# A hybrid decoder layer: gate one-hots on VectorE turned by ScalarE, gate products laid out key by token, and a gather rate of 0.8 in the second mixer half

## The chip, the cores and the metric

The kernel runs on one core of one Trainium2 chip. The metric is the device time of one execution in microseconds (us); the kernel before takes 3289.25 us (median of 3 runs, 3288.27 to 9417.04).

## The reference, cut to what matters

One decoder layer on 1024 tokens of width 1024, in float32:

```
z   = x @ W_in                                  # LRU input and gate, GLA q k v and gate, merge gates
m   = sigmoid(gA) * (RG-LRU(z) * gelu(z_y)) + sigmoid(gB) * (RMSNorm(GLA(z)) * silu(z_r))
x   = LN1(alpha * x + m @ W_out)
ple = sigmoid(x @ W_pg) * (p @ W_pp)
x   = LN2(alpha * x + PEER(x) + ple)
```

PEER has 8 heads. Each token's query picks, in each head, the top 16 of 128 keys in two halves, then the top 16 of the 256 pairs; a pair (i, j) names one of 16384 experts. Expert e adds g_e * v_e * gelu(u_e . x), where g is a softmax over the 16 picked. So every token has 128 experts, each with a row of 1024 numbers in the tables u and v.

## The kernel before, in words

The 1024 tokens are 8 tiles of 128, in two halves of 4 tiles. For each half `mixer` runs the projections, the LRU and the GLA, and `post` runs the output projection, LN1, the queries, the scores of the keys and the ple gates. PEER is computed in two ways. For four tiles (0, 1, 6, 7, `GT`) the picked rows are gathered from HBM: `gather_u` fetches one row per token (128 rows for one of the 128 picks) and one VectorE operation multiplies it with x and sums (line 849); `gather_v` fetches for one token its 128 value rows, and TensorE multiplies four tokens' rows with block-diagonal weights `w32`, in 8 phases of 16 gathers a tile. For the other four tiles (4, 5, 2, 3, `DT`) all 16384 experts are computed: `dense` runs u, gelu, a gate for every expert and v, as three products each (`mm3`) of numbers split into a high and a low part (`split`: ScalarE writes the high part, VectorE subtracts).

The gates of the dense tiles come from `dense_gates`. A token's 128 picks lie on the partitions. For each token `one` marks the picked i-key, `oi` is `one` times the gate, `oj` marks the picked j-key, and the product of `oj` and `oi` over the picks is the token's table of gates, j by i. 16 tokens are collected in `gst` and stored. Before the change VectorE makes `one` and `oj` for 8 tokens at a time, ScalarE makes `oi` token by token, and ScalarE evicts four tokens' products from PSUM with a turn from token-key to key-token order.

The order of work. Gathers, routes and value products are a stream (`gathers`) that weaves u, routes and v one after the other. The code of the main work calls `pump(t)`, which adds t times a rate to a credit and issues steps of the stream while the credit is positive (a gather costs 1.46, a route's selection 1.0 a key list). `RATE` has the rate for the first post, the second mixer half, the second post and the dense stage. Routes join the weave once 100 u gathers are issued (`ROUTE`), and v of a tile once its u are done. A planner then orders each engine's instructions at compile time from modelled times and priorities; in the second mixer half the stream is held behind the last VectorE instruction issued (`PIN`) and has a lower priority, in the dense stage a much higher one (`LATER`). Row buffers are a ring of 7, in the dense stage 11, for u and v together. All gathers are issued on GpSimd's (POOL's) queue, all other loads and stores on SP's. `GATES` says how many blocks of 16 tokens of dense gates are issued in each step of the second post: two after each of four column blocks of the output projection, one after each of the eight heads, four before each of four column blocks of the ple gate.

Weights are used by both halves. `weights` splits them in the first half and stores the low part in HBM for the first 60 keys (`LOW`); in the second half those low parts are loaded, and the others split again. By the order of the calls the 60 keys are all of the mixer's 56 and the first 4 of the output projection's 8; those of the queries (8), the ple gate (8) and the ple projection (4) are not stored.

Of the kernel before, what the change touches and what calls it, by code (L numbers as in the profile page):

```python
# [8 lines left out]
F32 = mybir.dt.float32  # L9
F32R = mybir.dt.float32r  # L10
BF16 = mybir.dt.bfloat16
I32 = mybir.dt.int32
U32 = mybir.dt.uint32
AF = mybir.ActivationFunctionType
# [4 lines left out]
P = 128  # L19
# [22 lines left out]


ROUTE = 100
RATE = (0.8, 0.6, 1.0, 1.2)

V = mybir.EngineType.DVE
PIN = ((), (V,), (), (None,))
# [5 lines left out]
KG = 4  # L54
RING = 6

LOW = 60

TG = 8

# [7 lines left out]
def kernel(ctx: ExitStack, tc: tile.TileContext, a: dict, out: bass.AP, tap=None):  # L68
# [198 lines left out]
    def weights(src, name, shape):  # L267
# [8 lines left out]
        if low.get(key) is not None:  # L276
            nc.sync.dma_start(l.bitcast(F32), low[key])
            nc.scalar.activation(h, raw, AF.Copy)
        else:
            split(h, l, raw)  # L280
            if key not in low:
                n = len(low)
                low[key] = None
                if n < LOW:
                    low[key] = dram.tile(shape, F32, name=f"low{n}")
                    nc.sync.dma_start(low[key], l.bitcast(F32))
        return h, l

    low = {}
# [567 lines left out]
    def gather_v(ti, idx, idxT, gate, H):  # L857
# [5 lines left out]
        for ph in range(32 // N):  # L863

            w32 = peer.tile([P, 4, N, 32], F32, name="w32", bufs=2)
            nc.vector.memset(w32, 0.0)
            for c in range(4):
                dst = w32[:, c].rearrange("p r e -> p (r e)")[:, ph * N:ph * N + (N - 1) * 33 + 1:33]
                nc.vector.tensor_copy(dst, pw[:, 32 * c + ph * N:32 * c + ph * N + N])
            for r in range(N):  # L870

                rows_v = []
# [89 lines left out]
    def dense_gates(n, g_b, gps, iota):  # L962
# [2 lines left out]
        o = gps.tile([P, 4, KEYS], F32, name="pk3", tag="g")  # L965
        for j in range(3):
            nc.tensor.transpose(o[:, j], K3[:, j], ident)
        T3 = g_b.tile([P, 3, P], F32, name="T3", bufs=2)
        nc.scalar.activation(T3, o[:, :3], AF.Copy)
        Tb = g_b.tile([P, 2, P], BF16, name="Tb", bufs=2)  # L970
        nc.scalar.activation(Tb, o[:, :2], AF.Copy)
        for tb in range(P // 16):
            gs = g_b.tile([P, KEYS, 16], F32, name="gst", tag="g")
            for q in range(16 // TG):
                t0 = tb * 16 + q * TG
                tt = slice(t0, t0 + TG)
                B3 = [P, TG, KEYS]
                one = g_b.tile(B3, BF16, name="one", bufs=2)
                nc.vector.tensor_tensor(one, iota, Tb[:, 0, tt, None].to_broadcast(B3), op=ALU.is_equal)  # L979
                oj = g_b.tile(B3, F32, name="oj", bufs=2)  # L980
                nc.vector.tensor_tensor(oj, iota, Tb[:, 1, tt, None].to_broadcast(B3), op=ALU.is_equal)  # L981
                for r4 in range(TG // 4):
                    o = gps.tile([P, 4, KEYS], F32, name="pg", tag="g")
                    for r in range(4):
                        t = 4 * r4 + r
                        oi = g_b.tile([P, KEYS], F32, name="oi", bufs=6)
                        nc.scalar.activation(oi, one[:, t], AF.Copy, scale=T3[:, 2, t0 + t:t0 + t + 1])  # L987
                        nc.tensor.matmul(o[:, r], oj[:, t], oi, start=True, stop=True)  # L988
                    q4 = q * TG + 4 * r4
                    nc.scalar.activation(gs[:, :, q4:q4 + 4].rearrange("p i t -> p t i"), o, AF.Copy)  # L990
                    pump(0.9)
            nc.sync.dma_start(g_d[:, :, n * P // 16 + tb].rearrange("g j i t -> j g (i t)"),
                              gs.rearrange("p (g i) t -> p g (i t)", i=8))
            yield
# [109 lines left out]
    with ExitStack() as gctx:  # L1104
        g_b = gctx.enter_context(tc.tile_pool(name="g_b", bufs=2))
        gps = gctx.enter_context(tc.tile_pool(name="gps", bufs=3, space=PSUM))

        iota = late.tile([P, TG, KEYS], BF16, name="iota", tag="tr")
        nc.scalar.activation(iota, iota128[:, None, :].to_broadcast([P, TG, KEYS]), AF.Copy)

        def all_gates():
            for n in (*range(ND, TT), *range(ND)):
# [75 lines left out]
```

## Time and profile before

| | before |
|---|---|
| median of 3 runs | 3289.25 us |
| the profiled execution's own time | 3298.0 us |
| its span, first to last instruction | 3296.2 us |
| mean granted TensorE clock, share of full speed | 0.954 |
| TensorE products busy | 3042.8 us (92%) |
| VectorE busy | 2375.3 us (72%) |
| ScalarE busy | 1228.2 us (37%) |
| GpSimd busy | 1160.8 us (35%) |

The span shows these stages: mixer half 0 from 0 to about 420 us, its post to 655, mixer half 1 to 1115, its post with the dense gates to about 1630, the dense stage to 3258, and a tail to 3296. Busy shares over the whole span mix these stages; each is read by itself. A busy TensorE counts products that overlap, so the times from start to start are used where a product's price is wanted.

### The profile page before, as it was taken

Reading aid. Unit: us, or ns where it says so; the run is one execution under the profiler, and the core shown is the slowest. Engines: PE = TensorE matmul, PEld = TensorE weight load, DVE = VectorE, ACT = ScalarE, POOL = GpSimd, SP = SyncE. Lnnn points to the kernel's source line nnn. Section 1 sums busy time; section 2 is a strip of 40 time slices with the busy share of each in tenths; the row PEclk is TensorE's granted clock in tenths of the full one; section 3 lists DMA queues with packets and bytes.
Section 4 is the critical chain, followed back from the end, with each engine's and each line's share of the span. In section 5 each row is a group of like instructions: output and inputs, shape, how many; then the busy total and the mean of one; then the engine's idle time right before and its main releaser. Section 6 shows DMA issues by size and latency. Waiting matters only on the chain.

```text
span 3296.2 us, 48127 instructions
## 1 busy us (share of the span) xinstructions
PE 3042.8 (92%) x17160; PEld 2320.6 (70%) x17160; DVE 2375.3 (72%) x5791; ACT 1228.2 (37%) x2130; POOL 1160.8 (35%) x1034
## 2 busy tenths in 40 slices
PE   8999989797999888658799999999999999999996
PEld 6788777676777676548577777777777777777663
DVE  7556557977888898978887866666666667666333
ACT  6433323263244464648623322222232232223221
POOL 0000000534421445540155444444434545443453
PEclk9999989898999998879899999999999999999997
DMA  5444444777776898976799899999899999988997
GB/s 174 143 172 148 135 160 142 277 293 284 295 263 244 326 312 302 349 252 216 246 376 352 321 338 327 340 338 344 314 340 326 355 335 326 338 328 327 346 322 277
DMA packets 364304, 939.74 MB, mean 285 GB/s; under 512 B 33920, under 2 KB 115968, under 8 KB 359968
## 3 DMA queue, kind: packets, MB, share of 16 engines
q0 software_dynamic: 147456, 536.94, 44.8%
q1 hardware_dynamic: 216608, 399.74, 34.8%
q8 instruction: 134, 2.20, 0.3%
q14 instruction: 106, 0.87, 0.1%
HBM read 854.76 MB, written 81.79 MB: 284 GB/s over the span
## 4 chain that ended last, share of the span: by engine, by line
PE 70%; DVE 14%; DMA 7%; ACT 4%; issue 3%; POOL 1%; SPq 0%; POOLq 0%; DVEq 0%; ACTq 0%
PE ph L263 7%; PE ph L265 7%; PE pv L265 7%; PE pv L263 7%; PE pv L264 7%; PE ph L264 7%; PE ffn L883 7%; DVE ug L849 3%; DMA ug<-in_peer_u_dram,idx 3%; DMA vg<-in_peer_v_dram,idxT 1%; DVE one L979 1%; DVE oj L981 1%; PE pgr L263 1%; PE pgr L264 1%; PE pgr L265 1%
## 5 line engine op out<-in xcount | busy, mean ns | idle before, releaser
L847 POOL DMA_INDIRECT ug<-in_peer_u_dram,idx x512 | 601.3, 1174 | 1345.1 <-DVE bs L776 612.3
L876 POOL DMA_INDIRECT vg<-in_peer_v_dram,idxT x512 | 558.2, 1090 | 756.7 <-DVE ug L849 324.3
L849 DVE SCALAR_TENSOR_TENSOR ug<-ug,x1g 128x1024 f32<-128x1024 f32 x512 | 619.8, 1219 | 47.0 <-DMA ug<-in_peer_u_dram,idx 42.9
L263 PE MATMUL ph<-x1hl,uh 128*128 128x512 f32 x1024 | 408.6, 399 | 0.9 <-DVE sc L737 0.9
L265 PE MATMUL ph<-x1hl,ul 128*128 128x512 f32 x1024 | 407.9, 398 | 0.0
L264 PE MATMUL ph<-x1hl,uh 128*128 128x512 f32 x1024 | 406.6, 397 | 0.0
L264 PE MATMUL pv<-vl,wdh 128*128 128x512 f32 x1024 | 400.5, 393 | 0.0
L263 PE MATMUL pv<-vh,wdh 128*128 128x512 f32 x1024 | 384.3, 393 | 15.9 <-ACT wdh L259 15.9
L265 PE MATMUL pv<-vh,wdl 128*128 128x512 f32 x1024 | 398.7, 393 | 0.0
L259 ACT ACTIVATE uh<-ur 128x512 fp32r<-128x512 f32 x256 | 160.2, 628 | 498.0 <-PE ph L264 489.2
L883 PE MATMUL ffn<-vg,w 128*32 128x512 f32 x2048 | 274.1, 628 | 51.1 <-DMA vg<-in_peer_v_dram,idxT 50.2
L259 ACT ACTIVATE vh<-vr 128x512 fp32r<-128x512 f32 x256 | 160.7, 629 | 356.9 <-PE pv L265 348.7
L260 DVE TENSOR_TENSOR ul<-ur,uh 128x512 fp32r<-128x512 f32 x256 | 175.7, 687 | 159.6 <-ACT uh L259 158.1
L260 DVE TENSOR_TENSOR vl<-vr,vh 128x512 fp32r<-128x512 f32 x256 | 176.3, 690 | 115.2 <-ACT vh L259 115.0
L1062 DVE SCALAR_TENSOR_TENSOR acc<-acc,pv 128x512 f32<-128x512 f32 x256 | 165.0, 681 | 108.8 <-PE pv L265 108.8
L263 PEld LDWEIGHTS pv<-vh,wdh 128*128 128x128 f32 x1024 | 192.8, 188 | 69.3 <-ACT wdh L259 16.1
L263 PEld LDWEIGHTS ph<-x1hl,uh 128*128 128x128 f32 x1024 | 192.4, 188 | 68.6 <-issue 22.6
L265 PEld LDWEIGHTS ph<-x1hl,ul 128*128 128x128 f32 x1024 | 192.4, 188 | 62.1 <-issue 16.8
L265 PEld LDWEIGHTS pv<-vh,wdl 128*128 128x128 f32 x1024 | 192.6, 188 | 58.7 <-issue 16.8
L264 PEld LDWEIGHTS ph<-x1hl,uh 128*128 128x128 f32 x1024 | 192.4, 188 | 55.7 <-issue 11.7
L264 PEld LDWEIGHTS pv<-vl,wdh 128*128 128x128 f32 x1024 | 192.9, 188 | 53.9 <-issue 10.1
L988 PE MATMUL pg<-oi,oj 128*128 128x128 f32 x1024 | 163.2, 301 | 35.9 <-ACT oi L987 25.4
(475 smaller groups left out, 6030.9 us busy)
## 6 DMA issues: line engine op xcount, KB each, us to landing
ur<-in_uT_dram SPq DMA_DIRECT2D x256, 256.0 KB, 6.3
vr<-in_peer_v_dram SPq DMA_DIRECT2D x256, 256.0 KB, 6.3
g_d<-gst SPq DMA_DIRECT2D x32, 1024.0 KB, 8.6
gt<-g_d SPq DMA_DIRECT2D x32, 1024.0 KB, 8.4
raw_zx<-in_w_z_dram SPq DMA_DIRECT2D x16, 512.0 KB, 4.9
raw_zv<-in_w_v_dram SPq DMA_DIRECT2D x16, 512.0 KB, 5.0
raw_zy<-in_w_z_dram SPq DMA_DIRECT2D x16, 512.0 KB, 6.4
raw_ga<-in_w_z_dram SPq DMA_DIRECT2D x16, 512.0 KB, 5.4
```

What stands on the lines that cost most here:

```text
L259: nc.scalar.activation(h, src, AF.Copy)
L260: nc.vector.tensor_tensor(l, src, h, op=ALU.subtract)
L263: nc.tensor.matmul(o, wh, xh, start=first, stop=False)
L264: nc.tensor.matmul(o, wh, xl, start=False, stop=False)
L265: nc.tensor.matmul(o, wl, xh, start=False, stop=last)
L847: nc.gpsimd.indirect_dma_start(out=ug, out_offset=None, in_=a["peer_u"], in_offset=bass.IndirectOffsetOnAxis(ap=idx[:, s:s + 1], axis=0))
L849: nc.vector.scalar_tensor_tensor(ug, ug, 1.0, x1, op0=ALU.mult, op1=ALU.mult, accum_out=hid[:, s:s + 1])
L876: nc.gpsimd.indirect_dma_start(out=vg, out_offset=None, in_=a["peer_v"], in_offset=bass.IndirectOffsetOnAxis(ap=idxT[:, t:t + 1], axis=0))
L883: mm = nc.tensor.matmul(ffn[32 * c:32 * c + 32, e * 512:(e + 1) * 512], w32[:, c, r], rows_v[c][:, e * 512:(e + 1) * 512], start=ph == 0 a ...
L979: nc.vector.tensor_tensor(one, iota, Tb[:, 0, tt, None].to_broadcast(B3), op=ALU.is_equal)
L988: nc.tensor.matmul(o[:, r], oj[:, t], oi, start=True, stop=True)
L1062: nc.vector.scalar_tensor_tensor(acc[c][:, es], acc[c][:, es], 0.5 if g == 0 else 1.0, o[c], op0=ALU.mult, op1=ALU.add)
```

## The change

Five edits. The rate of the second mixer half goes from 0.6 to 0.8. The low parts of all weights but the queries' (`pq`) are kept in HBM, where before the first 60 keys were. `w32` is cleared by GpSimd and filled by ScalarE, where VectorE did both. In `dense_gates`, VectorE marks the j-keys of 8 tokens in a key-token layout, ScalarE turns that to token-key order in float32 (`oj`), and VectorE makes the gated mark of the i-key in one operation per token (`oi`). The products are written to PSUM key by token, with a stride of four numbers, and the eviction copies them in that order.

```
-RATE = (0.8, 0.6, 1.0, 1.2)
+RATE = (0.8, 0.8, 1.0, 1.2)
...
-LOW = 60
+OWN = ("pq",)
...
-            if key not in low:
-                n = len(low)
-                low[key] = None
-                if n < LOW:
-                    low[key] = dram.tile(shape, F32, name=f"low{n}")
-                    nc.sync.dma_start(low[key], l.bitcast(F32))
+            if name not in OWN and key not in low:
+                low[key] = dram.tile(shape, F32, name=f"low{len(low)}")
+                nc.sync.dma_start(low[key], l.bitcast(F32))
...
             w32 = peer.tile([P, 4, N, 32], F32, name="w32", bufs=2)
-            nc.vector.memset(w32, 0.0)
+            nc.gpsimd.memset(w32, 0.0)
             for c in range(4):
                 dst = w32[:, c].rearrange("p r e -> p (r e)")[:, ph * N:ph * N + (N - 1) * 33 + 1:33]
-                nc.vector.tensor_copy(dst, pw[:, 32 * c + ph * N:32 * c + ph * N + N])
+                nc.scalar.activation(dst, pw[:, 32 * c + ph * N:32 * c + ph * N + N], AF.Copy)
...
-        T3 = g_b.tile([P, 3, P], F32, name="T3", bufs=2)
-        nc.scalar.activation(T3, o[:, :3], AF.Copy)
-        Tb = g_b.tile([P, 2, P], BF16, name="Tb", bufs=2)
-        nc.scalar.activation(Tb, o[:, :2], AF.Copy)
+        T2 = g_b.tile([P, 2, P], F32, name="T2", bufs=2)
+        nc.scalar.activation(T2, o[:, 0:3:2], AF.Copy)
+        Tb = g_b.tile([P, P], BF16, name="Tb", bufs=2)
+        nc.scalar.activation(Tb, o[:, 1], AF.Copy)
...
-                tt = slice(t0, t0 + TG)
-                B3 = [P, TG, KEYS]
-                one = g_b.tile(B3, BF16, name="one", bufs=2)
-                nc.vector.tensor_tensor(one, iota, Tb[:, 0, tt, None].to_broadcast(B3), op=ALU.is_equal)
-                oj = g_b.tile(B3, F32, name="oj", bufs=2)
-                nc.vector.tensor_tensor(oj, iota, Tb[:, 1, tt, None].to_broadcast(B3), op=ALU.is_equal)
+
+                one = late.tile([P, KEYS, TG], BF16, name="one", tag="k_", bufs=2)
+                nc.vector.tensor_tensor(one, iota, Tb[:, None, t0:t0 + TG].to_broadcast([P, KEYS, TG]), op=ALU.is_equal)
+                oj = g_b.tile([P, TG, KEYS], F32, name="oj", bufs=2)
+                nc.scalar.activation(oj.rearrange("p t k -> p k t"), one, AF.Copy)
+
+                oi = g_b.tile([P, TG, KEYS], F32, name="oi", bufs=2)
+                for t in range(TG):
+                    nc.vector.tensor_scalar(oi[:, t], iota128, T2[:, 0, t0 + t:t0 + t + 1], T2[:, 1, t0 + t:t0 + t + 1],
+                                            op0=ALU.is_equal, op1=ALU.mult)
                 for r4 in range(TG // 4):
-                    o = gps.tile([P, 4, KEYS], F32, name="pg", tag="g")
+                    o = gps.tile([P, KEYS, 4], F32, name="pg", tag="g")
                     for r in range(4):
                         t = 4 * r4 + r
-                        oi = g_b.tile([P, KEYS], F32, name="oi", bufs=6)
-                        nc.scalar.activation(oi, one[:, t], AF.Copy, scale=T3[:, 2, t0 + t:t0 + t + 1])
-                        nc.tensor.matmul(o[:, r], oj[:, t], oi, start=True, stop=True)
+                        nc.tensor.matmul(o[:, :, r], oj[:, t], oi[:, t], start=True, stop=True)
                     q4 = q * TG + 4 * r4
-                    nc.scalar.activation(gs[:, :, q4:q4 + 4].rearrange("p i t -> p t i"), o, AF.Copy)
+                    nc.scalar.activation(gs[:, :, q4:q4 + 4], o, AF.Copy)
                     pump(0.9)
...
-        iota = late.tile([P, TG, KEYS], BF16, name="iota", tag="tr")
-        nc.scalar.activation(iota, iota128[:, None, :].to_broadcast([P, TG, KEYS]), AF.Copy)
+        iota = late.tile([P, KEYS, TG], BF16, name="iota", tag="tr")
+        nc.scalar.activation(iota, iota128[:, :, None].to_broadcast([P, KEYS, TG]), AF.Copy)
```

## Rows read from the trace of the kernel before

**Rows 1.** Windows: stretch, length, busy by engine, granted clock, DMA share, GB/s

```profile
0.00:420.00 420.00, 403.13 (x2753) 320.65 (x2753) 264.63 (x647) 187.84 (x252) 1.34 (x10) 0.98 0.45 155
...
655.00:1115.00 460.00, 417.41 (x2754) 331.00 (x2752) 372.39 (x1045) 179.75 (x242) 150.17 (x123) 0.93 0.77 278
1115.00:1425.00 310.00, 238.26 (x1613) 184.69 (x1613) 290.71 (x836) 181.19 (x399) 159.29 (x122) 0.87 0.93 322
1425.00:1630.00 205.00, 154.15 (x1027) 138.82 (x1026) 174.65 (x473) 154.81 (x366) 38.77 (x31) 0.89 0.74 235
1630.00:3258.00 1628.00, 1628.00 (x7738) 1173.11 (x7740) 1075.35 (x2140) 459.21 (x769) 766.58 (x714) 1.00 0.92 335
3258.00:3296.20 38.20, 8.59 (x48) 1.32 (x36) 16.28 (x26) 1.36 (x5) 3.97 (x5) 0.55 0.61 225
```

**Rows 2.** Timeline of TensorE around one value group of the dense stage: start, length

```profile
2019.46 0.40 PE L263 MATMUL ph<-x1hl,uh 128*128 128x512 f32 x1
2019.70 0.40 PE L264 MATMUL ph<-x1hl,uh 128*128 128x512 f32 x1
2020.03 1.92 PE L883 MATMUL ffn<-vg,w 128*32 128x512 f32 x16
2021.88 0.50 PE L263 MATMUL pv<-vh,wdh 128*128 128x512 f32 x1
```

**Rows 3.** Chain of waits in the last 40 us: start, us, what

```profile
3262.25 11.20 DMA vg<-in_peer_v_dram,idxT
```

**Rows 4.** Windows of line 849 on VectorE (the u operations)

```profile
655.00:1115.00 460.00, 137.05 (x231) 0.93 0.77 278
1115.00:1630.00 515.00, 92.69 (x152) 0.88 0.86 287
```

**Rows 5.** Windows of line 876 on GpSimd (the issues of value gathers)

```profile
655.00:1115.00 460.00, 14.96 (x13) 0.93 0.77 278
1115.00:1630.00 515.00, 99.10 (x76) 0.88 0.86 287
```

**Rows 6.** VectorE's groups, 1115 to 1615: count, busy us, mean ns, idle before

```profile
L981 DVE TENSOR_TENSOR oj<-iota,Tb 128x1024 f32<-128x1024 bf16 x64 | 77.7, 1214 | 4.6 <-PE pg L988 4.6
L979 DVE TENSOR_TENSOR one<-iota,Tb 128x1024 bf16<-128x1024 bf16 x64 | 77.6, 1212 | 13.4 <-ACT oi L987 13.3
...
L260 DVE TENSOR_TENSOR wl_plg<-raw_plg,wh_plg 128x1024 fp32r<-128x1024 f32 x8 | 9.7, 1213 | 0.5 <-ACT wh_plg L259 0.4
...
L809 DVE TENSOR_TENSOR eq<-rb,iota 128x1024 bf16<-128x1024 bf16 x12 | 8.3, 688 | 0.2
...
L739 DVE FIND_INDEX8 i<-v,sc 128x8 uint32<-128x128 f32 x24 | 6.6, 283 | 0.0
...
L866 DVE MEMSET w<- 128x512 f32 x5 | 2.4, 485 | 0.3
...
L795 DVE TENSOR_SCALAR rkf<-rkf 128x128 f32<-128x128 f32 x3 | 0.9, 298 | 0.0
```

**Rows 7.** Chain of waits, 1320 to 1345: start, us, what

```profile
1336.94 1.14 DVE oj L981
```

**Rows 8.** VectorE's groups, 0 to 25: line 166 has a pointer scalar

```profile
L166 DVE TENSOR_SCALAR lmask<-i_f,jf 128x32 f32<-128x32 f32 x5 | 1.2, 241 | 0.1
...
L162 DVE TENSOR_SCALAR ish<-irow 128x32 int32<-128x32 int32 x5 | 0.8, 170 | 0.0
```

**Rows 9.** ScalarE's groups, 1115 to 1615

```profile
L987 ACT ACTIVATE oi<-one,T 128x128 f32<-128x128 bf16 x512 | 165.0, 390 | 41.2 <-DVE one L979 21.1 <-PE pg L988 19.9
L990 ACT ACTIVATE gst<-pg 128x512 f32<-128x512 f32 x128 | 133.3, 1054 | 14.0 <-DMA g_d<-gst 9.6 <-PE pg L988 4.2
L683 ACT ACTIVATE sc_st<-psc 128x512 f32<-128x512 f32 x16 | 8.8, 595 | 4.2 <-DVE list L739 4.2
```

**Rows 10.** TensorE's gate products

```profile
L988 PE MATMUL pg<-oi,oj 128*128 128x128 f32 x1024 | 163.2, 301 | 35.9 <-ACT oi L987 25.4 <-DVE oj L981 8.9 <-ACT gst L990 1.6
```

**Rows 11.** GpSimd's groups, 0 to 25

```profile
L214 POOL MEMSET qk<- 128x256 f32 x1 | 0.3, 302 | 0.0
```

## The prediction

> **What bounds the kernel now.** I read the windows by stage first [rows 1]. The reader should compare each stage's length with the busy columns. Mixer half 0 (0 to 420) runs with TensorE busy 403 us of 420 and no gathers. Mixer half 1 (655 to 1115) does the same matrix work in 460 us: without the 17 idle us of the first half, some 400 became 460. TensorE is busy 417 there, VectorE 372, and the granted clock is 0.93. The stretch 1115 to 1630 holds the second half's output projection, the queries, the routes and all four tiles' dense gates. In its first 310 us VectorE is busy 291, 94%; in its last 205 us nobody is near full (VectorE 175, ScalarE 155, TensorE 154), so there engines wait for each other in turn. From 1630 to 3258 TensorE is busy for all 1628 us at the full clock: the dense stage ends when TensorE has issued its list, and only a shorter list shortens it. The last 38 us are a tail.
>
> Then the order on TensorE inside the dense stage [rows 2]: products follow each other every 0.24 us, and one group of four gathered value rows (16 records) pushes the next product from 2019.94 to 2021.88, so it costs 1.94 us. Last the chain of waits at the end [rows 3]: a value gather that lands 11.2 us after its issue, behind the last dense product.
>
> How many gathers fall where: the u operation has two records a gather (product and accumulator), so 231 and 152 records [rows 4] are some 115 in mixer half 1 and 76 in the stretch after it. Value gathers: 13 and 76 [rows 5], so 423 of 512, 106 groups, are left for the dense stage.
>
> **The rate.** By the code, a mixer half calls for 345 credits (48 projections x 5.2, value projections 42, LRU 14, GLA chunks 40). At 0.6 that is 207, at 0.8 276: 69 more. At that point of the list one round is a u gather (1.46), a v gather (1.46) and a routing step (about 1.05), 3.97, so 17 more of each move into mixer half 1. The same arithmetic gives 138 u and 9 v by its end at 0.6, near the counts above. The 17 routing steps leave the next stretch, whose credits then buy 6 more u and 6 more v. The dense stage loses 23 of each: 6 groups x 1.94 = **-12 us**. The order of issue is fixed at compile time and u and v alternate, so 46 fewer gathers should put the last value group before the last product. Of the 38 us tail the wait until those rows land (3273.5) is 15.5, and the group behind them 2: I take **-17** (ends 0 and -22).
>
> Mixer half 1 pays. VectorE gets 17 u operations at 137.05/115.5 = 1.19 us, 20 us, and 17 routing steps at about five operations of 0.28 us [rows 6], 24 us: 44 us. The near end of the price: half 1 does some 190 us of u (137) and routing (by the code 37 steps, at 1.4) on VectorE and is 60 us longer, 0.32 us for each, so 44 cost 14. The far end: all 44, since VectorE would be busy 417 of 460. I take **+28**, between them, because VectorE passes 90% as it does in the first part of the next stretch. Four more value groups on TensorE (8 us) are inside it. Bytes: 34 gathers of 0.5 MB bring the 278 GB/s to about 300, under the 335 of the dense stage [rows 1], so on average transfers are no limit.
>
> **Kept low parts.** All weights but the queries' keep their low part in HBM: by the code 4 of the output projection, 8 gate and 4 projection keys are new. Post 1 loses 12 subtractions of 1.21 us [rows 6] and 4 of half the size: 17 us of VectorE. Post 0 stores 7.3 MB and post 1 reads it. On SP's queue a store waits for VectorE's subtraction, and behind it stand the raw weights of the next block. Nothing to 22 us each way (7.3 MB at 335 GB/s), **+3** taken: the first 60 keys are stored the same way in mixer half 0, where TensorE is at 96%.
>
> **The gates.** 64 turns of 8 tokens. VectorE before: two operations of 1.21 us a turn [rows 6], which in the chain follow each other after 1.14 [rows 7], an overlap of 0.08: 2.27 a turn. After: one comparison in the layout of the routing's own (1024 bf16, both inputs contiguous inside), 0.69 [rows 6], and eight tensor_scalar of 128 elements with two pointer scalars. No row has that form. With one pointer and 32 elements it is 0.24 against 0.17 without [rows 8]; with none and 128 elements 0.30 [rows 6]. So each is between 0.24 and 0.30 + 2 x 0.07 = 0.44; I take 0.32, near the 128-element row, as the add-ons partly overlap. Less 0.08: 0.61 + 8 x 0.24 = 2.53 a turn, +17 us over the 64; ends -24 and +78. ScalarE before: 8 x 0.39 + 2 x 1.05 = 5.2 us a turn [rows 9]. The eviction at 1.05 writes with a stride of 64 B; the contiguous one of the same 512 elements takes 0.60. The new evictions write runs of 16 B (0.60 each), and the turned copy of 1024 elements writes with a stride: 1.2 (twice 0.60) to 2.1 (twice 1.05), and I take 2.1, the strided row. That is 3.3 a turn, -1.9 x 64 = -122 us of ScalarE (ends -182 and, were the evictions still 1.05, -65).
>
> The gate products on TensorE are busy 163 us [rows 10]; they now write PSUM with a stride of 16 B, which no row has. I take no change, because each of a product's two records has 163.2/1024 = 0.16 us for 128 columns, where a dense product needs 0.24 for 512 [rows 2]: that is under half the pace per column, so a slower write has room. The Trainium skill (PSUM — Partial Sum Buffer, Specifications) says the opposite: PSUM cachelines are 8 bytes and "any non-contiguous AP slows matmuls significantly". By that rule the sum below is that of the second rival; no row shows which holds.
>
> **The block-diagonal w32.** VectorE loses 32 clears of 0.485 us [rows 6] and 128 tiny copies; in post 1 only 5 clears, -2 us. GpSimd gets 32 clears at about twice 0.30 us [rows 11], 19 us, between gathers, and is busy 767 of the dense 1628 [rows 1]; ScalarE gets the copies and is busy 459 there. Two waits are new: GpSimd's clear waits for the products that read the buffer two phases earlier, with gathers queued behind it, and ScalarE's copy waits for that clear, with the dense weight splits behind it, for which TensorE waits. Cover: the splits run ahead of TensorE by the three buffers of their pools. Taken at 0.
>
> **Post 1 in sum.** VectorE: -17 -24 +8 (6 u) -2 +17 = -18 of 466 us. ScalarE: -122 of 336. Where VectorE is 94% busy its net loss is nearly the stage's: -20. In the last 205 us the turn-taking chain shortens on ScalarE: -25, about half of what its 32 turns save (61). **-45**; ends -85 (both savings in full) and +20 (tensor_scalar at 0.44).
>
> Sum: +3 +28 -45 -12 -17 = **-43 us**. The profiled execution took 3298.0 us (span 3296.2), 9 above the median of 3289.25; the gain applied to the median gives **3246 us**.
>
> **Rivals.** *More is gained*: ScalarE's relief counts in full and mixer half 1 pays 18: 3 + 18 - 85 - 12 - 20 = -96, 3193. For it: no engine is full in 1425 to 1630. Against: VectorE hardly gets less.
> *Strided PSUM writes slow the gate products*: at half speed TensorE gets +163 us on 392 busy in 515. It has 123 idle, so from a factor of 1.75 on it is the bound; at 2 the stretch grows by 40 where I had it shrink by 45: 3246 + 85 = 3331, slower than before. For it: nothing in the trace writes so. Against: the slow pace per column above.
> *Mixer half 1 is full*: all 44 and 9 us of late u rows, on which VectorE's order of issue waits, post 1 -25, dense -12, no tail gain: 3 + 53 - 25 - 12 = +19, 3308. For: 91% on two engines.
> *GpSimd's late clears hold ScalarE*: 26 phases in the dense stage at 4 us beyond the buffers, +104 - 43: 3350. For: three queues in a row, all in order. Against: three buffers of splits.
> *The rate moves nothing*, if the compiled order already puts gathers where rows come free: 3 - 21 = 3271, inside the forecast's range.
>
> **Numbers.** Forecast 0.45 (its own range 3205 to 3285), more gained 0.22, mixer half full 0.14, strided writes 0.12, held ScalarE 0.07. 2% is 66 us, about what a measurement tells from no change. Faster than 3223: 0.22 and a fifth of the forecast's, 0.31. Slower than 3355: parts of the last two, 0.08. Within: 0.61. Range 3180 to 3335: it takes in the rivals up to the strided one and leaves out the far ends.
>
> **What would show it.** v gathers by 1115 near 30 instead of 13, and mixer half 1 at 475 to 505; dense stage 12 us shorter for the same products; last value group before the last product; ScalarE's busy time in post 1 near 215; tensor_scalar at 0.32; gate products still 163 us. Gate products at 300, or a TensorE that waits for ScalarE in the dense stage, would make it wrong.

## The result, and the profile after

The kernel after takes 3341.06 us (median of 4 runs, 3340.67 to 3344.09) against 3292.48 for the kernel before on the same chip (also 4 runs): a ratio of 1.0145 with an interval of 1.0128 to 1.0163. One run of the kernel before, of 9417.04 us, was slow and is left out of the ratio. The kernel after takes longer, by less than the 2% that the forecast took for a clear difference, but with the whole interval above 1; 3246 was forecast, and 3341 is 6 us above the range. The profiled executions took 3298.0 before and 3340.67 after, +43, where the sum was -43; the stages below account for these 43.

The windows of the kernel after, by its stages (columns as in [rows 1]; the borders are the starts of the first product of each kind, and the second row is the second post up to the first value product of the dense stage):

```profile
674.00:1176.00 502.00, 433.06 (x2826) 337.98 (x2826) 397.42 (x1180) 179.63 (x250) 173.94 (x150) 0.91 0.79 281
1176.00:1680.00 504.00, 368.73 (x2574) 308.86 (x2574) 439.04 (x1549) 257.75 (x324) 165.30 (x154) 0.86 0.89 301
1680.00:3321.00 1641.00, 1638.98 (x7761) 1183.77 (x7760) 1050.36 (x1997) 477.06 (x879) 755.84 (x714) 1.00 0.89 328
3321.00:3339.00 18.00, 0.22 (x1) 0.00 (x0) 13.92 (x23) 1.18 (x4) 0.00 (x0) 0.56 0.28 117
```

Cut at the same events, the kernel before has 665 (first post ends), 453, 510, 1629 and 39 us. So the 43 us are +9 up to the first post's end, +49 in mixer half 1, -6 in the second post, +12 in the dense stage and -21 in the tail. The gain expected from the second post is not there in its length, and the dense stage is longer although two value groups fewer fall into it.

VectorE's groups in the second post of the kernel after (columns as in [rows 6], which they answer):

```profile
L981 DVE TENSOR_SCALAR oi<-iota,T 128x128 f32<-128x128 f32 x496 | 136.1, 355 | 17.8 <-ACT T L966 10.6 <-PE pg L987 6.9
...
L975 DVE TENSOR_TENSOR one<-iota,Tb 128x1024 bf16<-128x1024 bf16 x64 | 43.6, 687 | 7.1 <-ACT oj L977 7.1
```

ScalarE's groups there, to compare with [rows 9]:

```profile
L977 ACT ACTIVATE oj<-one 128x1024 f32<-128x1024 bf16 x64 | 129.0, 2026 | 18.3 <-DVE one L975 9.7 <-PE pg L987 8.6
L989 ACT ACTIVATE gst<-pg 128x512 f32<-128x512 f32 x128 | 74.7, 606 | 75.6 <-PE pg L987 44.8 <-DMA g_d<-gst 28.8 <-issue 1.8
```

And TensorE's gate products, to compare with [rows 10]:

```profile
L987 PE MATMUL pg<-oi,oj 128*128 128x128 f32 x1024 | 145.6, 296 | 40.2 <-ACT oj L977 25.5 <-ACT gst L989 11.7 <-DVE oi L981 2.9
```

The marks with two pointer scalars take 355 ns, not 320; overlaps taken out they are busy 136.1/496 = 0.274 us each, 140 for all 512. With the 64 comparisons VectorE's marking takes some 184 us where it took 155 [rows 6]: +29, not +17. ScalarE did become cheaper, at the prices reckoned (2.03 and 0.61): 129 + 75 = 204 us instead of 298 [rows 9], -94. The products with strided writes are not slower: 145.6 us against 163.2.

At the end of the second post the order matters. TensorE's timeline of the kernel after (start, length; in brackets the idle time before and what ended it), where the gate products end at 1618 and the last ple projection at 1619:

```profile
1614.36 3.73 PE L987 MATMUL pg<-oi,oj 128*128 128x128 f32 x32
...
1625.97 3.64 PE L880 MATMUL ffn<-vg,w 128*32 128x512 f32 x16 [6.46 <-DMA vg<-in_peer_v_dram,idxT]
1650.84 1.92 PE L880 MATMUL ffn<-vg,w 128*32 128x512 f32 x4 [21.23 <-DMA gt<-g_d]
1665.69 0.80 PE L263 MATMUL ph<-x1hl,uh 128*128 128x512 f32 x1 [12.92 <-ACT uh L259]
```

TensorE stands still for 41 us here, though the dense stage's u products need no gates. Their weights (`ur`) come late, as SP's queue of the kernel after shows (start, us of issue):

```profile
1626.11 0.39 SPq L991 DMA_DIRECT2D g_d<-gst  x1
1626.59 8.39 SPq L721 DMA_DIRECT2D base_d<-tge  x4
1639.46 0.32 SPq L750 DMA_DIRECT2D sc<-sc_d  x1
1639.88 0.85 SPq L1026 DMA_DIRECT2D gt<-g_d  x2
1640.77 2.52 SPq L1068 DMA_DIRECT2D acc<-base_d  x4
1643.34 4.39 SPq L1010 DMA_DIRECT2D ur<-in_uT_dram  x3
```

The same view of the kernel before:

```profile
1549.40 0.37 SPq L992 DMA_DIRECT2D g_d<-gst  x1
1551.84 2.33 SPq L1011 DMA_DIRECT2D ur<-in_uT_dram  x3
...
1562.38 0.38 SPq L992 DMA_DIRECT2D g_d<-gst  x1
```

And TensorE's timeline of the kernel before, its first u product, its last gate products and its first value product:

```profile
1559.12 0.50 PE L263 MATMUL ph<-x1hl,uh 128*128 128x512 f32 x1
...
1611.28 1.07 PE L988 MATMUL pg<-oi,oj 128*128 128x128 f32 x6 [0.60 <-ACT oi L987]
1628.21 0.80 PE L263 MATMUL pv<-vh,wdh 128*128 128x512 f32 x1 [15.86 <-ACT wdh L259]
```

Before, the loads of the dense weights stand between the stores of the last gates, and 96 dense u products run while the gates are still made; TensorE then idles 15.9 us before the first value product. After, the loads are issued behind the last store and the last score load, and only 36 u products precede the first value product. The other 60 are done in the dense stage, at 0.24 us each [rows 2]: +14.

So the second post has two parts, and they went opposite ways. From its start (1118.7 before, 1175.7 after) to the end of the last gate product 493.7 us became 442.4: -51. From there to the first value product 15.8 us became 61.6: +46. VectorE is busy 447 us of the first part before and 395 after, 14 and 44 us of the second, so 30 us of its work only moved behind the gates. Yet VectorE is idle for 18 of those 62 us. The chain of waits of the kernel after names three loads there:

```profile
1622.97 10.52 DMA sc<-sc_d
...
1640.30 10.86 DMA gt<-g_d
...
1651.18 19.64 DMA vr<-in_peer_v_dram
```

They are a list of scores, gates read back and dense weights, 41 us in all. By this chain each is issued only when the one before it has landed, and after the scores VectorE's selection from them comes too.

The tail, in the chain of waits of the kernel after: the last dense product, and no gather behind it (the last one is issued at 3262):

```profile
3319.64 0.24 PE pv L265
3319.90 1.29 DVE acc L1061 x2
```

### The profile page after: what moved, and what is told of

The parts are those of the page before. It is cut to its first block, busy times and chain, and to the rows that moved or that the text cites. A ratio compares the mean times of both kernels' runs of the same rounds, so it can differ in the third digit from the quotient of the medians.

```text
span 3338.6 us, 48191 instructions
## 1 busy us (share of the span) xinstructions
PE 3045.9 (91%) x17160; PEld 2325.9 (70%) x17160; DVE 2364.5 (71%) x6063; ACT 1171.6 (35%) x1813; POOL 1143.8 (34%) x1066
## 4 chain that ended last, share of the span: by engine, by line
PE 73%; DVE 11%; DMA 8%; ACT 4%; issue 3%; POOL 0%; SPq 0%; DVEq 0%; ACTq 0%; POOLq 0%
PE ph L265 7%; PE ph L264 7%; PE ph L263 7%; PE pv L263 7%; PE pv L264 7%; PE pv L265 7%; PE ffn L880 7%; DVE ug L846 2%; PE pg L987 2%; DMA ug<-in_peer_u_dram,idx 2%; DMA g_d<-gst 2%; ACT oj L977 1%; PE ppq L263 1%; DMA sc<-sc_d 1%; PE pga L265 1%
## 5 line engine op out<-in xcount | busy, mean ns | idle before, releaser
L844 POOL DMA_INDIRECT ug<-in_peer_u_dram,idx x512 | 582.6, 1138 | 1450.4 <-DVE idxT L831 599.6
L873 POOL DMA_INDIRECT vg<-in_peer_v_dram,idxT x512 | 542.8, 1060 | 667.8 <-PE ffn L880 245.6
L1041 DVE TENSOR_TENSOR w<-w,gt 128x256 f32<-128x256 f32 x256 | 97.9, 422 | 123.0 <-ACT w L1038 123.0
```

Source lines behind the costliest of these rows:

```text
L844: nc.gpsimd.indirect_dma_start(out=ug, out_offset=None, in_=a["peer_u"], in_offset=bass.IndirectOffsetOnAxis(ap=idx[:, s:s + 1], axis=0))
L873: nc.gpsimd.indirect_dma_start(out=vg, out_offset=None, in_=a["peer_v"], in_offset=bass.IndirectOffsetOnAxis(ap=idxT[:, t:t + 1], axis=0))
L1041: nc.vector.tensor_mul(wq, wq, G[i // 8][q][:, :, i % 8])
```

## The experiments

Every ratio is to the kernel before on the same chip, as that kernel's own time differs by chip (medians of 3292 to 3315 us). Five theories are named in the expectations: A, the rate costs the time; B, the hand-over of `w32` from GpSimd to ScalarE does; C, the late start of the dense stage does; D, two chains, TensorE's and the gathers', end together, so that the long tail can be saved once only; V, VectorE's marks cost, because VectorE bounds the second post. R (the rate's price is paid back only where the tail is still long) came later. The table has all kernels, cut at the same events (us, from each trace); "gates" is the part of the second post up to the end of its last gate product, "VectorE" its busy time in the second post, "ahead" the number of dense u products before the first value product. Each row is one execution. The four `only_` rows, cheap_low_rate and cheap_all come from chips on which the kernel before takes 16 to 22 us longer than on the others, so a few us between their stages and those of other rows mean nothing; the ratios are free of that.

| kernel | ratio | first post ends | half 1 | second post | gates | VectorE | dense | tail | ahead |
|---|---|---|---|---|---|---|---|---|---|
| before | 1 | 665 | 453 | 510 | 494 | 460 | 1629 | 39 | 96 |
| after | 1.0145 | 674 | 502 | 504 | 442 | 439 | 1641 | 18 | 36 |
| only_rate | 0.9963 | 669 | 502 | 488 | 473 | 445 | 1628 | 18 | 96 |
| only_low | 0.9984 | 675 | 462 | 506 | 484 | 443 | 1629 | 39 | 96 |
| only_w32 | 0.9987 | 667 | 457 | 513 | 494 | 457 | 1630 | 40 | 96 |
| only_gates | 1.0034 | 667 | 460 | 525 | 478 | 479 | 1648 | 22 | 36 |
| no_gates | 1.0020 | 671 | 505 | 482 | 455 | 418 | 1629 | 18 | 72 |
| no_w32 | 1.0091 | 675 | 497 | 500 | 464 | 441 | 1640 | 18 | 36 |
| no_rate | 1.0058 | 673 | 459 | 501 | 458 | 438 | 1654 | 23 | 36 |
| no_low | 1.0176 | 664 | 500 | 523 | 465 | 456 | 1641 | 19 | 36 |
| onehots_only | 1.0085 | 665 | 456 | 524 | 480 | 481 | 1648 | 22 | 36 |
| layout_only | 0.9971 | 669 | 455 | 497 | 481 | 461 | 1628 | 39 | 96 |
| cheap_one | 0.9957 | 664 | 456 | 484 | 469 | 427 | 1629 | 40 | 96 |
| cheap_rate | 0.9953 | 666 | 494 | 467 | 442 | 406 | 1631 | 18 | 72 |
| cheap_low | 0.9949 | 672 | 458 | 477 | 455 | 412 | 1624 | 46 | 96 |
| cheap_low_rate | 1.0000 | 673 | 503 | 471 | 440 | 396 | 1647 | 18 | 36 |
| cheap_all | 1.0008 | 676 | 503 | 468 | 444 | 386 | 1650 | 18 | 36 |
| rate_04 | 1.0246 | 667 | 455 | 578 | 562 | 510 | 1629 | 39 | 96 |

Theory C is answered by the second post less its gates: 15 to 22 us in the eight kernels with 96 products ahead, 25 and 27 in the two with 72, 24 to 62 in the eight with 36. All six kernels with the new marks have 36, and so have two without them.

**The edits one by one**, and both kernels once more as a measure of the noise. The diffs are parts of the change above:

```
only_rate    RATE = (0.8, 0.8, 1.0, 1.2)
only_w32     nc.gpsimd.memset(w32, 0.0); nc.scalar.activation(dst, pw[...], AF.Copy)
only_low     if name not in OWN and key not in low:
only_gates   dense_gates(...) and iota as after
again_before, again_after   no edit
```

> The kernel before with the rate of the second mixer half at 0.8 and nothing else. Theory A (the rate costs what the change costs: 34 gathers and 17 routing steps more make mixer half 1 longer than they relieve later stages): mixer half 1 about 50 to 60 us longer than 460, the tail some 20 us shorter, in all +20 to +45 us. Theory B (the hand-over of w32 between GpSimd and ScalarE costs it): this run within 10 us of the kernel before. Theory C (the start of the dense stage, where SP's queue brings loads late, costs it, whatever edit moved the order): the time from the last gate product to the first dense value product, 16 us before and 62 us after, decides, and mixer half 1 alone does not.

> The kernel before with w32 cleared by GpSimd and filled by ScalarE, nothing else. Theory A: within 10 us of the kernel before. Theory B: +20 to +50 us, with ScalarE waiting some 90 us in all for GpSimd's clears and one long wait before the dense stage. Theory C: slower only if the gap between the last gate product and the first dense value product grows.

> The kernel before with the low parts of all weights but the queries' kept in HBM, nothing else. By the prediction 17 us less VectorE in the second post and 7.3 MB more stored and loaded: -15 to +5 us. Theories A and B say the same of it.

> The kernel before with the new gates of the dense tiles and nothing else. By the prediction VectorE about +17 us in the second post and ScalarE some -120 us: -10 to -30 us. If the 355 ns that the gated marks took in the changed kernel weigh on VectorE, 0 to +15 us. By theory C the gap at the start of the dense stage could grow here too.

> The kernel before once more, so that its profile stands on the same chip as the next three. Every theory: ratio 1.00, and the stages of the first profile within some 10 us each.

> The changed kernel once more on this chip. Every theory: ratio 1.010 to 1.016, if the parts' sum (0.996 x 0.999 x 1.003 x 0.998 = 0.996) missed something that the parts do together; near 1.00 if chips differ in what the change costs.

Repeated, the kernels gave 0.9998 (0.9981 to 1.0015) and 1.0148 (1.0126 to 1.0170). The single ratios are 0.9963, 0.9987, 0.9984 and 1.0034, with intervals of 0.001 to 0.002 either way; their product is 0.997. No edit alone loses more than 11 us, all together lose 1.45%: the parts don't add, and A (+20 to +45 us for only_rate) and B (+20 to +50 for only_w32) are wrong as single causes. In only_gates the prediction's -10 to -30 us did not come, the other reading's 0 to +15 did. Its second post is 15 us longer, but its last gate product comes 16 us earlier (478 against 494); behind that TensorE has one wait, for the late dense weights, which the view of waits of only_gates shows (total us, times, longest):

```profile
PE ph L263 <- ACT uh L259: 31.7, 1, 31.7
```

**One edit left out of the whole.** Each is the kernel after with the lines of that edit as before:

```
no_gates   dense_gates(...) and iota as before
no_w32     nc.vector.memset(w32, 0.0); nc.vector.tensor_copy(dst, pw[...])
no_rate    RATE = (0.8, 0.6, 1.0, 1.2)
no_low     LOW = 60
```

> The changed kernel with the gates of before (rate, low parts and w32 as changed). Theory D (TensorE's chain and the gathers' chain end together in the kernel before: what delays TensorE is hidden until some 20 us, and the tail can be saved once only): the rate saves the tail, the gates' delay of some 30 us then shows in full, so without the gates the ratio is 0.995 to 1.004. Theory B (w32's hand-over, which holds ScalarE before the dense stage): still 1.008 or more.

> The changed kernel with w32 cleared and filled by VectorE as before. Theory B (ScalarE held 90 us by GpSimd's late clears, 30 of them just before the dense stage): 1.000 to 1.006 instead of 1.015. Theory D with the gates at fault: 1.012 to 1.016, within 5 us of the changed kernel, because dense loads arrive late in that gap anyway.

> All edits but the rate (0.6 again in the second mixer half). Theory R (the rate's price is paid back only where the tail is still long): the rate adds 49 us to mixer half 1 and takes 22 from the second post and 21 from the tail; with the new one-hots the tail is short without it (22 us alone), so in the whole it costs 49 - 22 - 4 = some 23 us. Expected: mixer half 1 near 460, second post near 525, tail near 20 to 25, and 1.005 to 1.009 of before. Rival (the rate is neutral here too, as it was alone at 0.996, and the one-hots with the w32 hand-over explain the loss): 1.013 to 1.016, the second post at 525 or longer and the tail near 39.

> All edits but the kept low parts (the first 60 keys again). Neutral theory: first post 7 to 10 us shorter, mixer half 1 with its output and the second post longer by as much (VectorE has the 17 us of subtractions again, in a stage that it bounds): 1.012 to 1.017 of before. Rival (the stores of the low parts in the first post are a pure cost): 1.010 to 1.012, second post not longer than 504. Second rival (the low parts are the one edit that helps where VectorE bounds): second post 515 to 525, 1.018 to 1.021.

Against 1.0145, leaving out the gates gives back 0.0125 (no_gates has 1.0008 to 1.0033: 41 us), the rate 0.0087 (1.0039 to 1.0078: 29 us), `w32` 0.0054 (1.0066 to 1.0116: 18 us); leaving out the low parts loses 0.0031 (1.0150 to 1.0201), which is within the noise. no_gates and no_rate came as D and R expected, except that no_rate's second post was to be 525 and is 501. no_w32 came between the ranges of B (1.000 to 1.006) and D (1.012 to 1.016), and no_low between two of its three. This is where D is seen: the rate's 49 us in mixer half 1 buy 22 us of second post and 21 of tail in only_rate, but in the whole the tail is 23 without the rate and 18 with it, so that 5 is all it saves there, and the second post is 501 without and 504 with; the dense stage is 13 shorter with it. The windows of the second post of no_gates:

```profile
1176.00:1658.00 482.00, 382.34 (x2612) 319.06 (x2612) 417.57 (x1109) 335.39 (x777) 200.70 (x158) 0.90 0.95 317
```

With the old marks ScalarE is busy 335 us instead of 258, VectorE 418 instead of 439, and the stage is 22 us shorter and the dense stage 12. Yet the last gate product comes later with the old marks, after 455 us against 442, at the same VectorE time up to there (395 us in both, with ScalarE at 323 and 249). The loss through the new marks lies behind it: 62 us instead of 27 to the first value product, and 36 products ahead instead of 72.

**The gates taken apart.** layout_only writes the products key by token and keeps the old marks; onehots_only has the new marks with the old layout; cheap_one has the new layout and makes `one` with the cheap comparison, from which ScalarE gates the marks as before:

```
layout_only    +o = gps.tile([P, KEYS, 4], ...)   +nc.tensor.matmul(o[:, :, r], oj[:, t], oi, ...)
               +nc.scalar.activation(gs[:, :, q4:q4 + 4], o, AF.Copy)
onehots_only   dense_gates as after, but these three lines as before
cheap_one      layout_only, and
               +one = g_b.tile([P, KEYS, TG], BF16, ...)  # iota in this order too
               +nc.vector.tensor_tensor(oj, iota128[:, None, :].to_broadcast(B3), T3[:, 1, tt, None].to_broadcast(B3), ...)
               +nc.scalar.activation(oi, one[:, :, t], AF.Copy, scale=...)
```

> The kernel before with the key-token layout of the gate products and its eviction in that order, but the one-hots as before. If VectorE's 512 gated marks (0.355 us each in the changed kernel, +30 us on an engine that is 90% busy in the second post) are what the gates cost: -5 to -25 us, ScalarE's evictions 0.6 instead of 1.05 us. If strided PSUM writes or a moved start of the dense stage cost it: 0 to +15 us, as with all of the gates' edit.

> The kernel before with the new one-hots (VectorE's gated marks, ScalarE's turned copies) but the products laid out and evicted as before. Theory V (VectorE's marks cost: +30 us on the engine that bounds the second post): ratio 1.003 to 1.008, VectorE's busy time in the second post about 480 us, as with the whole edit. If the moved start of the dense stage alone is the cost and it came with the layout: 0.995 to 1.00.

> The key-token layout of the products with one more edit: VectorE compares the i-keys of 8 tokens in key-token order (0.69 instead of 1.21 us a turn, 34 us less in all), ScalarE makes the gated marks from it with a stride of 16 B, the j-marks stay on VectorE at 1.21. Theory V (VectorE's time is what the second post takes): 15 to 30 us below the kernel with the layout alone in the second post, ratio 0.985 to 0.994, less where the tail of gathers (39 us) grows with it. If ScalarE binds the second post: no gain or a loss, since its strided reads take longer than 0.39.

The layout gains (0.9961 to 0.9980), the marks lose (1.0068 to 1.0102), and the kernel that takes 33 us from VectorE and gives ScalarE 17 more gains (0.9942 to 0.9972): it beats the kernels before and after. V had the direction of all three, but not the size of the last: 0.985 to 0.994 was expected, with a second post 15 to 30 us below layout_only's, and it is 14 below. The window of onehots_only's second post:

```profile
1121.00:1645.00 524.00, 367.41 (x2576) 303.58 (x2573) 480.84 (x1733) 301.17 (x303) 173.70 (x154) 0.87 0.83 280
```

And of cheap_one's:

```profile
1121.00:1604.00 483.00, 394.59 (x2617) 319.58 (x2615) 427.13 (x1305) 347.60 (x756) 179.26 (x152) 0.90 0.91 302
```

ScalarE's busy time is lower in the longer one. VectorE's 54 us of difference go with 41 of the stage, but only 11 of the 41 lie before the last gate product (480 against 469); 29 lie behind it (44 against 15). onehots_only has its last gate product 14 us earlier than the kernel before. So V, which says that the marks' price on VectorE makes the stage longer, and C, which says that the late dense loads do, come together in every kernel with the new marks. No run keeps the loads in their place with the new marks, and how much of the loss is V's is not shown.

**A lower rate.**

```
-RATE = (0.8, 0.6, 1.0, 1.2)
+RATE = (0.8, 0.4, 1.0, 1.2)
```

> The kernel before with the rate of the second mixer half at 0.4, the other way: some 24 u and 9 v gathers and 23 routing steps fewer there. Theory D (two chains end together): mixer half 1 some 25 to 40 us shorter and the last dense product earlier, but the gathers end later, a tail of 70 us or more instead of 39, ratio 1.003 to 1.02. If only TensorE's chain counts: 0.990 to 0.998.

1.0246 (1.0227 to 1.0266), beyond D's 1.003 to 1.02, and neither of D's signs came: mixer half 1 was to be 25 to 40 us shorter and the tail 70 us or more, and it is 38. Ten v and nine u gathers fewer by the end of mixer half 1, and that half is not shorter (455 against 453): there they were free. They come back in the second post, because by its end 89 v and 217 u are issued in both kernels:

```profile
1122.00:1700.00 578.00, 411.60 (x2669) 331.70 (x2669) 509.50 (x1504) 334.02 (x766) 217.32 (x171) 0.86 0.82 273
```

VectorE has 50 us more there than before, and the stage is 68 longer, all of it before the last gate product (562 against 494). So the price of a step on VectorE is nothing in mixer half 1 between the rates of 0.4 and 0.6, and about its duration or more in the second post. This is V without C, as 96 products are ahead in both.

**Do the good parts add up?** cheap_one with one or two of the other edits; cheap_all adds `w32`, which makes it the whole change but for the new marks:

```
cheap_rate       cheap_one, RATE = (0.8, 0.8, 1.0, 1.2)
cheap_low        cheap_one, if name not in OWN and key not in low:
cheap_low_rate   both
cheap_all        both, and w32 as after
```

> cheap_one (key-by-token products, the i-key's comparison in the cheap layout, ScalarE gating the marks as before) with the rate of 0.8. Theory R: cheap_one has a tail of 40 us, so the rate is paid back as in only_rate: +49 in mixer half 1, -22 in the second post, -21 in the tail, 3273 + 6 = about 3279 in the span, 0.994 to 1.000 of before. If VectorE's time sets the second post (theory V): its length again follows VectorE's busy time there (near 400 us busy, 455 to 465 long). Rival (the shares of cheap_one and only_rate multiply): 0.990 to 0.993.

> cheap_one with all low parts kept but the queries'. Theory V: VectorE loses 17 us in the second post, which is 10 to 20 us shorter (465 to 475), the first post 8 to 10 us longer, so 0.992 to 0.996 of before. Rival (the loads of 7.3 MB of low parts cost the second post what the subtractions save): second post 484 or longer, 0.996 to 1.000.

> cheap_one with the kept low parts and the rate of 0.8: the change without its new one-hots and without the w32 hand-over. Theory V (VectorE's busy time sets the second post): from cheap_rate's 406 us busy and 467 long, 17 us of subtractions fewer, so some 390 busy and 450 to 458 long; first post 8 us longer, mixer half 1 near 496, tail 18: 0.990 to 0.996 of before. Rival (ScalarE, 350 us busy there, takes over the bound): second post 465 to 475, 0.997 to 1.001.

> The same with the w32 hand-over too, so the whole change but for the new one-hots. If w32 costs the whole some 19 us because ScalarE waits for GpSimd's clears, whatever the one-hots: 0.996 to 1.002, second post 5 to 10 us longer than in cheap_low_rate, ScalarE waits 50 us or more for the clears. If it costs only together with the new one-hots: within 0.002 of cheap_low_rate.

cheap_rate 0.9953 (0.9937 to 0.9970) is theory R's case: half 1 +38, second post -16, tail -22, dense +2 against cheap_one. cheap_low is 0.9949 (0.9936 to 0.9962). Neither can be told from cheap_one, and both together are no gain at all: 1.0000 (0.9988 to 1.0012), where V expected 0.990 to 0.996 and a second post of 450 to 458. V fails here. VectorE is busy 396 us only and the second post is still 471:

```profile
1176.00:1647.00 471.00, 385.94 (x2580) 313.13 (x2577) 395.64 (x1159) 343.24 (x751) 172.70 (x153) 0.89 0.96 325
```

The expectation's rival, ScalarE as the bound, had 465 to 475 and 0.997 to 1.001, and both numbers came. But ScalarE is busy 343 us of the 471, and 348 in cheap_one's 484, so its time hardly moves with the stage. The transfers are nearer to their end, at a DMA share of 0.96 and 325 GB/s, and may be the next bound below some 400 us of VectorE's time; no run takes transfers away, so neither is shown. What is plain is the dense stage: only 36 u products run ahead of the first value product again, and it is 1647, 16 us longer than cheap_rate's, about what the two ratios differ by. The lost head start isn't tied to the new marks. `w32` costs nothing that can be told from noise without the new marks (1.0008 against 1.0000, and 0.9987 alone), so its 18 us are a loss only together with them.

## Why the prediction was wrong, point by point

**The step that failed** is the sum of the second post with the dense stage behind it: -45 and -12 were forecast, -6 and +12 came. The -45 is made of VectorE's and ScalarE's work alone, and up to the last gate product it was near: -51. The way from there to the first value product has no term; it was put at nothing without a reason. It took +46 (61.6 us against 15.8) and left 60 u products, +14, to the dense stage. It is partly luck that -51 is so near -45, as 30 us of VectorE's work went behind the gates. Three things are in it.

*VectorE's marks.* The price of 0.32 us, chosen near the row without pointers, was 0.355, and with the overlap the marks add 29 us, not 17. The range given (0.24 to 0.44) held it. VectorE's sum of -18 came out at -21 all the same, for other reasons: alone, the rate takes 15 us from VectorE in this stage, the low parts 17, `w32` 3, and the gates add 19. The 19 is below 29 because in only_gates 16 of the 512 marks lie ahead of the stage's start (4 us) and seven splits of dense weights fall behind its end (5 us). (The sum's own 8 us for six u operations of 1.19 should have been 7.)

*ScalarE's relief.* Some -25 of the -45 was given to it, because in the last 205 us no engine was full [rows 1]. That was too much. ScalarE lost 72 us (330 to 258), not 122: 5.2 us a turn counts overlapping operations twice, 333 us in all where they were busy 298 [rows 9]. And the 72 count for little: layout_only takes 42 us of ScalarE and shortens the stage by 13, cheap_one gives back 60 and shortens it by another 14, as VectorE has 33 fewer. At the same VectorE time up to the last gate product, 74 us less of ScalarE brought that product 13 us forward (no_gates against after). A stretch in which nobody is full on the average isn't one where each engine's saving counts by half; the prices are found by taking the work away.

*The head start.* The prediction named a list on TensorE that only gets shorter. It also starts earlier or later: the u products that run among the gates belong to that list, and the planner placed 96 of them there before and 36 after. The 60 products make the +14; two value groups fewer between the first and the last value product give 4 back, and 2 us more of TensorE's idle time are added, which is the +12. That the planner reorders whole loads when costs change was not in the sum. What in its priorities decides between 96, 72 and 36 was not tried and stays open; it changed with the marks, and with rate and low parts together.

**The rate.** The counts were right: 29 v gathers by the end of mixer half 1 (30 forecast) and 158 u, for 13 and 141. The price was 49, not 28 (the stage's 502 us lie inside the 475 to 505 that were named as its sign). VectorE is busy 397 us for 366 in the same cut. TensorE's busy time grew by 19, its idle time by 29. Its projections waited 20 us for low parts loaded from HBM, against 5, and the GLA's products for VectorE's `AT` 26 us, against 18.5. The kernel after, TensorE's groups in mixer half 1:

```profile
L265 PE MATMUL pzy<-xhl,wl_zy 128*128 128x512 f32 x64 | 26.9, 425 | 5.4 <-DMA wl_zy<-low 5.4
...
L558 PE MATMUL po<-AT,v 128*128 128x128 f32 x64 | 15.2, 324 | 26.0 <-DVE AT L553 26.0
```

"On average transfers are no limit" was true, at 281 GB/s, and said nothing of single loads that come late. The rival "mixer half 1 is full", at +53, had this stage right. rate_04 shows why a price by proportion missed: from 0.4 to 0.6 a gather there is free, from 0.6 to 0.8 it isn't. The six u and six v gathers more that the second post was to take did not come either: it issues 74 of each, where it issued 76.

**The dense stage's six groups.** Fourteen v gathers more, not 23, were issued by the end of the second post. Four groups more run in mixer half 1 and one more in the second post; of these five about half left the tail, so between first and last value product two groups are gone, not six.

**The tail.** -17 was forecast, -21 came, with the mechanism named: the last gather is issued 58 us before the last product (3262 and 3320). What was missed is that a later end of TensorE's list gives the same gain: only_gates has a tail of 22 at the old rate. So the tail's part of the rate's pay lapses when something else delays TensorE.

**Low parts.** +3 was forecast for the first post and +9 came (665 to 674); it goes with this edit (675 in only_low, 664 in no_low), and that the stores make it is not shown. VectorE's -17 was right. Alone the edit is 0.9984 (0.9967 to 1.0001), and in the whole it can't be told from nothing either.

**`w32`, taken at 0.** The two waits are there. The line of the kernel after in the view of waits (total us, times, longest):

```profile
ACT w L866 <- POOL w L863: 89.7, 21, 29.6
```

The longest, on ScalarE's timeline of the kernel after:

```profile
1618.13 0.60 ACT L989 ACTIVATE gst<-pg 128x512 f32<-128x512 f32 x1 [0.30 <-PE pg L987]
1648.29 0.49 ACT L866 ACTIVATE w<-pw 128x4 f32<-128x4 f32 x4 [29.56 <-POOL w L863]
1665.00 0.63 ACT L259 ACTIVATE uh<-ur 128x512 fp32r<-128x512 f32 x1 [16.22 <-DMA ur<-in_uT_dram]
```

In the dense stage, where the rival at 3350, the nearest to the measured time, saw 26 phases at 4 us, ScalarE waits 45 us in 16 times and TensorE doesn't, so the cover named there held. The longest wait lies just ahead of the dense stage, where the next thing ScalarE does is wait for the late weights anyway. Of the 18 us that it costs with the new marks the profile shows half, 5 us of mixer half 1 and 4 of the second post (no_w32 against after; no_w32's profiled run took 3332 us, 4 above its median). In no_w32 the last gate product comes 22 us later and the way behind it is 25 us shorter; which wait makes the 18 is not shown.

**Strided PSUM writes**, the rival at 3331, near the measured time, is not the cause. In layout_only, with the same marks as before, the strided products are busy 155.2 us at 294 ns each, against 163.2 and 301 [rows 10], where they follow each other the usual step is 0.112 us in both, and the kernel gains. The rule of the Trainium skill (PSUM — Partial Sum Buffer, Specifications) that any non-contiguous access slows matmuls significantly doesn't show at these products' pace, so the trace disagrees with it here.

## What to carry to other kernels

Cut a stage at the event that the next one waits for, and read both parts: here the gates were done 51 us sooner and nothing came of it, because the loads of the next stage stood behind them. A compile-time order may put such loads elsewhere when costs change, and the lost head start then stands in the next stage's length. Price a move between two engines by taking work off each in turn, with the rest of the order in view. Edits measured alone need not add: two that shorten the same tail are paid for it once.

## What the runs showed of the hardware

A 128x128 tensor_scalar with two pointer scalars took 0.355 us, 0.274 with the overlap of its neighbours taken out; without pointers it took 0.298 [rows 6]. ScalarE took longer with strides on either side: the turned copy of 1024 elements took 2.03 us, the eviction 0.61 with runs of 16 bytes and 1.05 turned [rows 9], and in cheap_one the marks read at a stride of 16 bytes took 0.520 us for 128 elements, against 0.390 [rows 9]:

```profile
L987 ACT ACTIVATE oi<-one,T 128x128 f32<-128x128 bf16 x512 | 232.0, 520 | 41.2 <-PE pg L988 24.9 <-DVE one L979 16.1
```

TensorE's gate products were not slower for the 16 bytes from one number that they wrote to the next: 0.294 us against 0.301, in layout_only.
